# The last convolution block: where two squares stand in ScalarE's queue, and which engine makes two of its sums

## The chip, the cores and the metric

The kernel runs on one core of a Trainium2 chip. The core has TensorE (PE in the profile: matrix products into the accumulators called PSUM), VectorE (DVE), ScalarE (ACT), GpSimd (POOL) and SyncE (SP), each with an instruction queue of its own that it works off in order, and 16 DMA engines that move data between the chip's large memory and SBUF, the memory beside the engines. The metric is the time of one execution on the device in microseconds; with several runs, their median.

## The reference, cut to what matters

One layer of an encoder: 2048 positions, width 1024. Half of the projected columns are Fourier-mixed, the other half go through two gated long convolutions (Hyena).

```python
h = rmsnorm(x)
p = h @ w_in                       # 2048 x 2048: [Fourier 512 | x1 512 | x2 512 | v 512]
y_f = rmsnorm(real(fft2(p[:, :512] in 8 groups of 64)))
x1, x2, z = split(short_conv(p[:, 512:]))
for n, gate in enumerate((x1, x2)):
    z = gate * irfft(rfft(z, 4096) * k_freq[n])[:2048] + skip term
y_h = rmsnorm(z)
x = x + concat(y_f, y_h) @ w_out
x = x + relu(rmsnorm(x) @ w_fc1)**2 @ w_fc2
out = rmsnorm(x)
```

## The kernel before

The stages follow one another: input projection with the short convolution; the filters' spectra and the Fourier mix, both left in the chip's memory; the eight blocks of long convolutions (`hyena`, L744); the output projection (`project_out`); the two products of the feed-forward part. The change touches `hyena` and the class `Out`, which prepares the output projection.

**A convolution block.** A `Block(n, ct)` is the convolution `n` (two of them) of 128 of the 512 channels. The transform is done in two factors by matrix products. `first` makes the first factor and turns its result on VectorE. `second(q)`, q = 0 to 7, takes a group of four frequencies: it makes the second factor on TensorE into PSUM (L797) and multiplies by the filter's spectrum `ks`. A complex product needs the two halves of the rows swapped and one of them negated: ScalarE makes that swapped copy `zs` in two instructions (L800 the negated half, L801 the other). VectorE makes `y = p * ks[0]` (L803), GpSimd `zs = zs * ks[1]` (L804), and the two are summed into `y` (L805). In blocks 0 to 6 GpSimd makes the sums of q = 0 to 3 and VectorE those of q = 4 to 7; in the last block (number 7) GpSimd makes those of q = 0 and 1 and VectorE those of q = 2 to 7. `inverse(q)` multiplies `y` back on TensorE, and ScalarE copies the product into `V` (L814). `turn` turns `V` into `W` on VectorE, in eight pieces. `gate(q)` makes the last factor on TensorE (L826), and VectorE multiplies it by the gate `xg` into `zz` (L827).

**How blocks overlap.** In one pass over q, the block at hand goes through `second` and, three groups later (`LAG`), `inverse`; the block before it ends its `inverse` and is turned; the block before that is gated. Behind the loop the last block's inverse products of q = 5 to 7, the gates of block 6, and the turns and gates of block 7 are left.

**What is begun early for the output projection.** Behind `second(1)` of the last block, `Out.ahead` (L954, a generator that goes on at each `next`) loads the Fourier rows of two token tiles (`yf`, two transfers of 128 KB each per tile, L928 and L930), before the spectra of q = 4 to 7. Its second part is called at q = 7: for each of the two rows the mean of squares (`rms`, L237: the square on ScalarE at L240, with its sum read by a second, short instruction; then short steps on VectorE and a square root on ScalarE) and the scaling of the row on ScalarE (L962). Later parts transpose the rows on TensorE (L937), split them in two parts of reduced precision (`split`, L193 to L201; the cast `yh` on ScalarE, the rest `yl` on VectorE) and multiply them with `w_out` (L211 to L213). The weights of `w_out` (`ost`) are split on ScalarE and VectorE or GpSimd (`weights`, L911) before that. Their transfers take the buffers of the spectra that have been used.

**What sets the order.** The text above is not the order of the queues. The tile framework orders each engine's instructions itself when the program is built, from the dependences, the order of the text and a time model of its own; an instruction from further down may so come ahead. `behind(later, first)` (L203) adds an edge without a wait: `later` is placed behind `first` in the order. `squared` holds the last square that `rms` has issued. Before the change nothing ties the two squares of the Fourier rows to a place.

Of the kernel before, what the change touches and what calls it, by code (L numbers as in the profile page):

```python
# [134 lines left out]
def hybrid_block(ctx: ExitStack, tc: tile.TileContext, A, out):  # L135
    nc = tc.nc
# [36 lines left out]
    def pa(nm):  # L173
        banks["n"] += 1
        pl, tag = (ps, "a") if banks["two"] or banks["n"] % 2 else (banks["other"], "b")
        return pl.tile([P, 512], F32, tag=tag, name=nm, bufs=4)
# [26 lines left out]
    def behind(later, first):  # L203

        order = mybir.DependencyInfo(mybir.DependencyClass.NoSync, mybir.DependencyReason.DATA)
        for x in later:
            tc.add_manual_dep(x.ins, first.ins.name, order, reason="queue order")
# [7 lines left out]
    def rsqrt(v, pl, nm, keep=None, s=None):  # L215

        r = pl.tile(list(v.shape), F32, tag=f"rc_{nm}", name=f"rc_{nm}")
        q = pl.tile(list(v.shape), F32, tag=f"nw_{nm}{keep or ''}", name=f"nw_{nm}", bufs=keep)
        if s is None:
            s = pl.tile(list(v.shape), F32, tag=f"sq_{nm}", name=f"sq_{nm}")  # L220
            nc.scalar.sqrt(s, v)
        nc.vector.reciprocal(r, s)
        if v.shape[1] == 1:

            nc.vector.tensor_scalar(out=q, in0=r, scalar1=r, scalar2=v, op0=ALU.mult, op1=ALU.mult)
            nc.vector.tensor_scalar(out=q, in0=q, scalar1=-0.5, scalar2=1.5, op0=ALU.mult, op1=ALU.add)
            nc.vector.tensor_scalar(out=q, in0=q, scalar1=r, scalar2=None, op0=ALU.mult)
            return q
        nc.vector.tensor_mul(q, r, r)
        nc.vector.tensor_mul(q, q, v)  # L230
        nc.vector.tensor_scalar(out=q, in0=q, scalar1=-0.5, scalar2=1.5, op0=ALU.mult, op1=ALU.add)
        nc.vector.tensor_mul(q, r, q)
        return q

    squared = []

    def rms(src, width, junk, nm, keep=None):  # L237

        ssq = small.tile([P, 1], F32, tag="ssq", name=f"ssq_{nm}")
        squared[:] = [nc.scalar.activation(junk, src, AF.Square, accum_out=ssq)]  # L240
        v = small.tile([P, 1], F32, tag="var", name=f"v_{nm}")
        nc.vector.tensor_scalar(out=v, in0=ssq, scalar1=1.0 / width, scalar2=EPS, op0=ALU.mult, op1=ALU.add)
        return rsqrt(v, small, "s", keep)
# [106 lines left out]
    def doubled(i, q):  # L350

        both = kd[i // 2][i % 2].rearrange("h p s x -> h (p s) x")[:, :, 1024 * q : 1024 * q + 1024]
        behind([nc.sync.dma_start(both[1], both[0])], fetched[0])
# [390 lines left out]
    def hyena(hp, wp, rp, zz, e1, b1, f2, a2, work):  # L744
# [6 lines left out]
        class Block:  # L751
# [41 lines left out]
            def second(self, q):  # L793
                ks = self.ahead.pop(q) if q in self.ahead else self.spectrum(q)
                p = pa("pz2")
                for j in range(4):
                    nc.tensor.matmul(p[:, 128 * j : 128 * j + 128], lhsT=f2[q // 4][:, 4 * (q % 4) + j, :], rhs=self.G[:, :, 4 * q + j], start=True, stop=True)  # L797
                p3 = p.rearrange("p (f c) -> p f c", f=4)
                zs = hp.tile([P, 4, 128], F32, tag="zs", name="zs", bufs=4)
                nc.scalar.mul(zs[0:64], p3[64:128], -1.0)  # L800
                nc.scalar.copy(zs[64:128], p3[0:64])  # L801
                y = hp.tile([P, 4, 128], F32, tag="y", name="y", bufs=5)
                nc.vector.tensor_mul(y, p3, ks[:, 0])  # L803
                nc.gpsimd.tensor_mul(zs, zs, ks[:, 1])  # L804
                (nc.gpsimd if q in ((0, 1) if self is blocks[7] else (0, 1, 2, 3)) else nc.vector).tensor_add(y, y, zs)  # L805
                self.y[q] = y

            def inverse(self, q):
# [12 lines left out]
            def gate(self, q):  # L821
# [6 lines left out]
                    zz[:, 4 * q : 4 * q + 4, self.cs], p.rearrange("p (t c) -> p t c", t=4), self.xg[:, 4 * q : 4 * q + 4, :]  # L828
                )

        LAG = 3
        TURNS = ((0,), (1,), (2, 3), (4, 5), (6, 7))
        LAST = ((0,), (1, 2), (3, 4), (5, 6), (7,))
        FIRSTS = ((0, 1), (2, 3), (4,), (5,), (6,), (7,), (), ())
        blocks = [Block(n, ct) for n in range(2) for ct in range(4)]
# [7 lines left out]
        for i in range(8):  # L843
            cur, old, older, new = (blocks[j] if 0 <= j < 8 else None for j in (i, i - 1, i - 2, i + 1))
            for q in range(8):
                if new and q == 7:
                    new.ahead[0] = new.spectrum(0)
                cur.second(q)
                if older and q == 1:
                    for k in range(4):  # L850
                        older.gate(k)
                if old:
                    if q < LAG:
                        old.inverse(8 - LAG + q)
                    else:
                        for c in (TURNS if new else LAST)[q - LAG]:
                            old.turn(c)
                if q >= LAG:
                    cur.inverse(q - LAG)
                if old and q == 3:  # L860
                    old.load()
                if i == 7:
                    if q == 1:
                        cur.ahead.update((k, cur.spectrum(k)) for k in range(2, 4))
                        ahead = work.ahead(hp, cur.y[0][:, 0, 0:1])
                        next(ahead)
                        cur.ahead.update((k, cur.spectrum(k)) for k in range(4, 8))
                    elif q == 5:
                        for k in range(4):
                            work.load(hp, k)  # L870
                    elif q == 7:
                        next(ahead)
                    elif q == 6:
                        cur.load()
                if new:
                    for c in FIRSTS[q]:
                        new.first(c)
                if 1 <= i < 5 and q % 2:
                    doubled(SINGLE[i - 1], q // 2)
        old, older = blocks[7], blocks[6]  # L880
        for q in range(8 - LAG, 8):
            old.inverse(q)
        for k in range(0, 4):
            work.weights(hp, k)
        for q in range(4):
            older.gate(q)
        next(ahead)
        for c in range(8):
            old.turn(c)
# [10 lines left out]
    class Out:  # L900
# [53 lines left out]
        def ahead(self, hp, late):  # L954

            rows, fronts = [], []
            for t in tokens[0:2]:
                rows.append(self.fourier_rows(t, hp, "yf", 2, late))
            yield
            for y in rows:  # L960
                junk = hp.tile([P, 512], BF16, tag="yjunk", name="yjunk")
                nc.scalar.mul(y, y, rms(y, 512, junk, "f"))  # L962
            yield
            for t, yn in zip(tokens, rows):
                fronts.append(self.parts(yn, *(hp.tile([P, 4, P], F32, tag="y", name=n, bufs=5).bitcast(FR) for n in ("yh", "yl")), t))
            yield
            for t, f in zip(tokens, fronts):
                self.begun[t] = [pa("po") for _ in range(2)]
                for h in range(2):
                    self.multiply(self.begun[t][h], f, 0, h)  # L970
                yield
# [573 lines left out]
    with pool("raws") as rp:  # L1545
        with pool("wts") as wp:
            work = Out(wp, zp, zz, gy)
            with pool("hyena") as hp:
                hyena(hp, wp, rp, zz, e1z, b1, f2h, f2, work)
            tabs.close()  # L1550

            raws = rp.tile([P, 32, 128], F32, tag="W", name="W").rearrange("p (n f) c -> p n (f c)", n=4)
            b = {}
            with pool("op") as op:
                first = project_out(op, work, raws, b)
            with pool("fc1") as mp:
                begun = fc1(mp, raws, zp, b, *first)
        zstack.close()
# [55 lines left out]
```

## Time and profile before

| | |
|---|---|
| median of 3 runs | 2241.47 us (2239.9 to 2246.95) |
| the profiled execution: its time | 2239.05 us |
| the profiled execution: its span, first to last instruction | 2237.3 us |
| mean TensorE clock granted | 0.996 |
| busy share of the span | PE 98%, DVE 66%, ACT 48%, POOL 34% |
| the last block's `second`, q = 0 to its last sum | about 756 to 780.5 us |

The page gives busy times by engine over the whole span, the same in 40 slices, the DMA queues, a chain of waits, the costliest groups of instructions and the transfers' issues. The time lines quoted below give start, duration, engine, line, operation and tiles, how many instructions were merged (x2), and in brackets the idle time of that engine just before and what ended it. Durations of neighbouring instructions overlap a little, since one begins while the other's last results are written; where a queue is full, the difference of two starts is the time that an instruction takes.

### The profile page before, as it was taken

How to read it: one execution, taken by the hardware profiler on the slowest of the kernel's cores; microseconds unless marked ns; L12 is line 12 of the kernel's file. 1: busy time of each engine (PE TensorE's matmuls, PEld its weight loads, DVE VectorE, ACT ScalarE, POOL GpSimd, SP SyncE). 2: the span in 40 equal slices, each digit the busy share in tenths (PEclk: the TensorE clock that was granted, in tenths of full speed). 3: DMA queues.
4: the chain of work that ended last, by engine and by line, in shares of the span. 5: the costliest groups of instructions: out<-in, count | busy, mean ns of one | idle time of the engine just before them, and what ended most of it. 6: DMA issues, size and time to landing. Idle time of an engine off the chain costs nothing. (4 is left out here: it accounts for less than half of the span.)

```text
span 2237.3 us, 34489 instructions
## 1 busy us (share of the span) xinstructions
PE 2192.4 (98%) x12881; PEld 1793.3 (80%) x12881; DVE 1468.4 (66%) x2192; ACT 1072.4 (48%) x1783; POOL 762.3 (34%) x576
## 2 busy tenths in 40 slices
PE   8999899999999999999999999999999999999998
PEld 6888778676888778887888878888888888888886
DVE  6998767776788764467444464444476666866667
ACT  6554211355555654546555565555443333533333
POOL 3444323465366511327555446555200000000000
PEclk9999999999999999999999999999999999999999
DMA  8534797569998756586444465444498756866631
GB/s 266 177 134 159 268 335 295 191 218 350 314 306 260 234 161 183 169 265 211 155 156 155 155 238 167 153 146 151 160 381 297 242 188 197 305 194 189 199 111 76
DMA packets 287001, 475.95 MB, mean 213 GB/s; under 512 B 17573, under 2 KB 131439, under 8 KB 282097
## 3 DMA queue, kind: packets, MB, share of 16 engines
q1 hardware_dynamic: 280593, 458.22, 61.5%
q10 hardware_dynamic: 6240, 15.53, 2.1%
q8 instruction: 101, 1.65, 0.3%
q14 instruction: 67, 0.55, 0.1%
HBM read 312.51 MB, written 168.00 MB: 215 GB/s over the span
## 5 line engine op out<-in xcount | busy, mean ns | idle before, releaser
L197 ACT CAST qahm<-ra 128x1024 fp32r<-128x1024 f32 x110 | 115.9, 1053 | 345.0 <-PE p2u L212 171.7
L197 DVE TENSOR_TENSOR qalm<-ra,qahm 128x1024 fp32r<-128x1024 f32 x110 | 134.7, 1224 | 153.4 <-ACT qahm L197 151.7
L1379 POOL TENSOR_TENSOR acc<-acc,gfin 128x512 f32<-128x512 f32 x4 | 5.1, 1282 | 630.2 <-DMA out<-acc 624.4
L212 PE MATMUL pu<-wl,xh 128*128 128x512 f32 x512 | 201.9, 394 | 6.9 <-DVE wl L197 6.5
L211 PE MATMUL pu<-wh,xh 128*128 128x512 f32 x512 | 204.9, 400 | 2.6 <-ACT wh L201 2.6
L213 PE MATMUL pu<-wh,xl 128*128 128x512 f32 x512 | 201.8, 394 | 2.7 <-DVE xl L197 2.7
L212 PE MATMUL p2u<-qblm,qahm 128*128 128x512 f32 x504 | 196.1, 389 | 0.0
L211 PE MATMUL p2u<-qbhm,qahm 128*128 128x512 f32 x504 | 195.8, 389 | 0.0
L213 PE MATMUL p2u<-qbhm,qalm 128*128 128x512 f32 x504 | 195.8, 389 | 0.0
L197 DVE TENSOR_TENSOR qblm<-rb,qbhm 128x1024 fp32r<-128x1024 f32 x110 | 134.0, 1218 | 2.2 <-ACT qbhm L197 2.2
L421 POOL TENSOR_TENSOR acc<-acc,cw 128x512 f32<-128x512 f32 x45 | 60.9, 1354 | 197.5 <-DVE acc L398 194.3
L212 PEld LDWEIGHTS pu<-wl,xh 128*128 128x128 f32 x512 | 97.4, 190 | 28.8 <-DVE wl L197 6.9
L197 ACT CAST ahm<-s 128x512 fp32r<-128x512 f32 x120 | 74.4, 621 | 94.1 <-PE p1v L212 54.8
L197 ACT CAST qbhm<-rb 128x1024 fp32r<-128x1024 f32 x110 | 115.3, 1048 | 4.4 <-DMA rb<-in_w_fc 2.9
L213 PEld LDWEIGHTS pu<-wh,xl 128*128 128x128 f32 x512 | 97.2, 190 | 24.4 <-DVE xl L197 4.1
L211 PEld LDWEIGHTS pu<-wh,xh 128*128 128x128 f32 x512 | 97.4, 190 | 23.8 <-ACT wh L201 3.5
L197 POOL TENSOR_TENSOR alm<-W,ahm 128x512 fp32r<-128x512 f32 x60 | 83.3, 1390 | 86.8 <-ACT ahm L197 86.8
L211 PEld LDWEIGHTS p2u<-qbhm,qahm 128*128 128x128 f32 x504 | 94.6, 188 | 20.1 <-issue 0.3
L213 PEld LDWEIGHTS p2u<-qbhm,qalm 128*128 128x128 f32 x504 | 94.6, 188 | 19.8
L212 PEld LDWEIGHTS p2u<-qblm,qahm 128*128 128x128 f32 x504 | 94.6, 188 | 19.5
L1155 DVE TENSOR_TENSOR c<-p1v,ku 128x512 f32<-128x512 f32 x64 | 44.2, 690 | 89.9 <-ACT ku L1225 51.2
L197 POOL TENSOR_TENSOR alm<-s,ahm 128x512 fp32r<-128x512 f32 x60 | 92.2, 1537 | 29.6 <-ACT ahm L197 29.6
(379 smaller groups left out, 6148.9 us busy)
## 6 DMA issues: line engine op xcount, KB each, us to landing
ks<-spec SPq DMA_DIRECT2D x64, 512.0 KB
W<-in_w_fc SPq DMA_DIRECT2D x64, 512.0 KB
rb<-td SPq DMA_DIRECT2D x64, 512.0 KB
ra<-a1m SPq DMA_DIRECT2D x56, 512.0 KB
ra<-a0m SPq DMA_DIRECT2D x54, 512.0 KB
rb<-in_w_fc SPq DMA_DIRECT2D x46, 512.0 KB
f<-in_w_fc SPq DMA_DIRECT2D x16, 1024.0 KB
td<-f SPq DMA_DIRECT2D x16, 1024.0 KB
```

Of the source, the lines that this page charges most:

```text
L197: return nc.scalar.copy(hi, src), eng.tensor_sub(lo, src, hi)
L211: a = nc.tensor.matmul(o, lhsT=lh, rhs=rh, start=start, stop=False, skip_group_check=more)
L212: nc.tensor.matmul(o, lhsT=lh, rhs=rl, start=False, stop=False, skip_group_check=more)
L213: return a, nc.tensor.matmul(o, lhsT=ll, rhs=rh, start=False, stop=stop, skip_group_check=more)
L421: nc.gpsimd.tensor_add(m1, m1, cw[:, 3, :])
L1155: read["DVE"] = nc.vector.tensor_add(c, p, other)
L1379: nc.gpsimd.tensor_mul(acc[i][:, c], acc[i][:, c], gfin[:, c])
```

## The change

In the last block the sums of q = 3 and 5 go from VectorE to GpSimd as well (four on GpSimd, four on VectorE). And the two squares of the Fourier rows are tied behind the second half (L801) of the swapped copy of q = 6: `swapped` holds the copy that `second` issued last, the loop notes it at q = 6, and at q = 7 it places both squares behind it. `ahead` therefore collects both squares in `squared`. Nothing else changes; no transfer and no product is added or left out.

```diff
-                nc.scalar.copy(zs[64:128], p3[0:64])
+                swapped[:] = [nc.scalar.copy(zs[64:128], p3[0:64])]
...
-                (nc.gpsimd if q in ((0, 1) if self is blocks[7] else (0, 1, 2, 3)) else nc.vector).tensor_add(y, y, zs)
+                (nc.gpsimd if q in ((0, 1, 3, 5) if self is blocks[7] else (0, 1, 2, 3)) else nc.vector).tensor_add(y, y, zs)
...
+        swapped = []
...
+                    elif q == 6:
+                        last = swapped[0]
+                        cur.load()
                     elif q == 7:
                         next(ahead)
-                    elif q == 6:
-                        cur.load()
+                        behind(squared, last)
...
+            both = []
             for y in rows:
                 junk = hp.tile([P, 512], BF16, tag="yjunk", name="yjunk")
                 nc.scalar.mul(y, y, rms(y, 512, junk, "f"))
+                both += squared
+            squared[:] = both
```

## The prediction

> **What bounds the kernel now.** I read the page first, for the shares of the engines; then TensorE's waits behind the changed stage; then the time line of each engine in the last convolution block (about 752 to 805 us), since the diff touches nothing else.
>
> ```profile
> span 2237.3 us, 34489 instructions
> PE 2192.4 (98%) x12881; PEld 1793.3 (80%) x12881; DVE 1468.4 (66%) x2192; ACT 1072.4 (48%) x1783; POOL 762.3 (34%) x576
> ```
>
> TensorE (PE) is the bound of the whole: 2237.3 less 2192.4 leaves 45 us in which it does nothing, and no edit of order can win more than the part of these 45 us that lies where it acts. The change removes no matmul. So the question is which idle time of PE in the last block depends on ScalarE (ACT), VectorE (DVE) and GpSimd (POOL). First the stall that the change is aimed at, in the time line of ACT, DVE, POOL and PE (start, duration, engine, line, what; in brackets the idle time before and what ended it):
>
> ```profile
> 762.55 1.06 PE L797 MATMUL pz<-G,f2h 128*128 128x128 f32 x8
> 762.75 0.60 ACT L814 COPY V<-pv 128x512 f32<-128x512 f32 x1 [1.94 <-PE pv L813]
> 765.94 0.63 ACT L240 ACTIVATE yjunk<-yf 128x512 bf16<-128x512 f32 x1 [2.59 <-DMA yf<-yfd]
> 766.69 0.59 ACT L800 ACTIVATE zs<-pz 64x512 f32<-64x512 f32 x1
> 767.29 0.58 ACT L801 COPY zs<-pz 64x512 f32<-64x512 f32 x1
> 766.70 0.15 DVE L242 TENSOR_SCALAR v_f<-ssq_f 128x1 f32<-128x1 f32 x1 [4.33 <-ACT yjunk L240]
> 767.90 0.69 DVE L803 TENSOR_TENSOR y<-pz,ks 128x512 f32<-128x512 f32 x1 [1.05 <-ACT zs L801]
> 767.95 1.29 POOL L804 TENSOR_TENSOR zs<-zs,ks 128x512 f32<-128x512 f32 x1 [4.86 <-ACT zs L801]
> 770.11 1.13 PE L813 MATMUL pv<-y,f 128*128 128x128 f32 x8 [1.14 <-DVE y L805]
> ```
>
> The product of the third group of frequencies (q = 2) is ready on PE at 762.55 + 1.06 = 763.61. ACT, which must negate and swap its halves (L800, L801), stands from 763.35 to 765.94 before the square of a Fourier row whose transfer has not landed. So 765.94 - 763.61 = 2.33 us are lost for ACT; DVE and POOL, which wait for the swapped copy, lose 4.33 and 4.86 us, and PE, which had run ahead, pays 1.14 us at 770.11 and more after it.
>
> Next, the end of the stage:
>
> ```profile
> 768.50 0.62 ACT L240 ACTIVATE yjunk<-yf 128x512 bf16<-128x512 f32 x1
> 769.22 0.59 ACT L800 ACTIVATE zs<-pz 64x512 f32<-64x512 f32 x1
> 777.23 0.58 ACT L801 COPY zs<-pz 64x512 f32<-64x512 f32 x1
> 787.17 0.60 ACT L197 CAST yh<-pt_y 128x512 fp32r<-128x512 f32 x1
> 779.86 0.65 DVE L805 TENSOR_TENSOR y<-y,zs 128x512 f32<-128x512 f32 x1
> 781.06 1.16 PE L813 MATMUL pv<-y,f 128*128 128x128 f32 x8
> 787.82 0.50 PE L211 MATMUL po<-G,yh 128*128 128x512 f32 x1 [0.76 <-ACT yh L197]
> 790.20 3.07 DVE L492 STREAM_TRANSPOSE W<-V 128x512 f32<-128x512 f32 x5
> 793.52 1.94 PE L826 MATMUL pb<-W,b 128*64 128x512 f32 x8
> core 0: us, PE busy (x) PEld busy (x) DVE busy (x) ACT busy (x) POOL busy (x), PEclk, DMA share, GB/s
> 766.00:787.00 21.00, 17.16 (x115) 12.43 (x113) 18.54 (x37) 20.65 (x35) 9.71 (x7) 1.00 0.81 268
> ```
>
> From 766 to 787 ACT is busy for 20.65 of 21.00 us: after its stall it never waits again until the first cast of a transposed Fourier row (787.17), and PE's first output product starts right behind that cast, 0.76 us late. This full queue of ACT is the bound here. The other chain ends earlier: the last sum on DVE (779.86 + 0.65 = 780.51), PE's last inverse product (781.06), block 6's gates.
>
> **The change, part by part.** *Squares behind the seventh swapped copy.* Nothing is removed. Each square takes ACT's queue for 0.75 and 0.72 us (765.94 to 766.69, 768.50 to 769.22), 1.47 us together; they now come behind the copy of q = 6. The negated copy of q = 2 then starts when PE has its product, at 763.61 instead of 766.69, 3.1 us earlier; those of q = 3 to 6 are 2.33 + 1.47 = 3.8 us earlier; that of q = 7 is 2.33 us earlier with both squares ahead of it (775.5 for the end of its copy instead of 777.23 + 0.58 = 777.8), and up to 3.8 if the scheduler puts them behind it. I take 2.33. The rows have landed long before, so the squares wait for no transfer in their new place. What is late next is ACT's own list: its work from 765.94 to 787.17, 21.2 us, begun at 763.61, ends at 784.8, and the yh cast comes 2.33 us earlier. The scale factors that the rows need (three short DVE steps, then ACT) are made late in any case, behind the sums:
>
> ```profile
> 780.50 0.13 DVE L242 TENSOR_SCALAR v_f<-ssq_f 128x1 f32<-128x1 f32 x1
> 784.97 0.20 DVE L227 TENSOR_SCALAR nw_s<-nw_s,rc_s 128x1 f32<-128x1 f32 x1
> 784.99 1.36 ACT L962 ACTIVATE yf<-yf,nw_s 128x512 f32<-128x512 f32 x2
> ```
>
> The second row's mean square is read at 780.50, 11 us after its square (768.50 + 0.62), so squares that end some 4 us later, near 774, cost nothing there unless DVE's order changes (a rival, below).
>
> *Two sums from DVE to POOL.* The groups of operations between 760 and 790 us (count; busy time, mean ns; idle time before them):
>
> ```profile
> L804 POOL TENSOR_TENSOR zs<-zs,ks 128x512 f32<-128x512 f32 x7 | 9.2, 1314 | 8.3 <-ACT zs L801 7.7 <-DVE G L492 0.6
> L805 DVE TENSOR_TENSOR y<-y,zs 128x512 f32<-128x512 f32 x6 | 4.1, 685 | 0.0
> L492 DVE STREAM_TRANSPOSE G<-V 128x512 f32<-128x512 f32 x8 | 5.6, 703 | 0.0
> L805 POOL TENSOR_TENSOR y<-y,zs 128x512 f32<-128x512 f32 x2 | 2.6, 1280 | 0.2
> ```
>
> From 767.90 to 780.51 DVE issues 20 large operations without a pause (6 products, 8 turns, 6 sums): 12.6 us, 0.63 each. Two fewer save 1.26 us of DVE; its list, begun at 764.8, would be through at 764.8 + 11.35 = 776.2, so DVE is no longer the bound. POOL gets 2 x 1.28: six products and two sums are 6 x 1.314 + 2 x 1.28 = 10.4 us, from 764.8 to 775.2, beside a last product that cannot start before 775.5. So POOL can hold it, with little room; each sum itself comes 1.28 - 0.69 = 0.6 us later than on DVE. Its readers are the inverse products of q = 3 and 5. The last sum (q = 7, still on DVE) ends at 775.5 + 1.31 + 0.65 = 777.5 instead of 780.51: 3.0 us earlier. That is 0.7 us more than ACT's gain, and the smaller of the two counts: **2.3 us**.
>
> *Transfers.* No new ones; but faster readers could run into them.
>
> ```profile
> 763.40 2.71 SPq L776 DMA_DIRECT2D ks<-spec  x4
> 766.00:772.00 6.00, 4.86 (x43) 4.64 (x41) 4.21 (x8) 5.86 (x13) 2.58 (x2) 1.00 1.01 345
> ```
>
> The spectra of q = 4 to 7, 512 KB each, are issued just behind the Fourier rows. With the rows landed at 765.94 and 345 GB/s, 1.52 us each, they land at my estimate at 767.5, 769.0, 770.5 and 772.0. The swapped copies would be there at 768.5, 770.3, 772.2 and 775.5, so the spectra are 1.0 to 3.5 us early. I cost them at nothing; without that cover the chain of the sums has 0.7 us of slack.
>
> *What follows.* The stage's later steps (turns to 793.27, gates at 793.52, output products) hang on the yh cast and on the last inverse product and shift as a whole. TensorE's largest waits from 803 us on are these (us in total, times, longest):
>
> ```profile
> PE p1u L211 <- ACT ku L1225: 2.1, 3, 1.0
> PE p1u L211 <- ACT bm L197: 1.6, 1, 1.6
> PE po L211 <- ACT oyh L197: 0.9, 2, 0.7
> ```
>
> None is for a transfer directly; all are for work that follows PE's own results, so nothing there should swallow the gain. Sum: 2239.05 us of the profiled execution less 2.3 is 2236.7. That execution lies 2.4 us below the median of the three runs (2241.47); the middle of all four executions (2239.05, 2239.9, 2241.47, 2246.95) is 2240.7, and I forecast **2240.7 - 2.3 = 2238.4 us**.
>
> **Rivals.** *DVE and POOL block each other* (the gain goes). The trace has the row:
>
> ```profile
> 610.14 2.96 POOL L804 TENSOR_TENSOR zs<-zs,ks 128x512 f32<-128x512 f32 x2 [1.26 <-DVE y L803]
> 610.15 1.81 DVE L805 TENSOR_TENSOR y<-y,zs 128x512 f32<-128x512 f32 x1
> ```
>
> A DVE sum of two SBUF operands that starts 0.01 us behind a POOL product takes 1.81 us instead of 0.69, 1.1 more. In the block as it is, POOL pauses (8.3 - 4.86) / 6 = 0.57 us before a product, and DVE's sums fall into those pauses (mean 685 ns). With POOL nearly full, the four sums left on DVE have few pauses: at worst 4 x 1.1 = 4.5 us, DVE through at 780.7, the gain of the sums' chain gone. It decides from 0.7 us on, so from the first blocked sum; two of them leave 2.3 - 1.5 = 0.8 us. Result between 2239.9 and 2240.9. For it speaks POOL's 10.4 us in a stretch of 12; against it, that the two moved sums are two fewer that can be blocked. The Trainium skill, in "SBUF — State Buffer" under "Who interferes with whom", says that a DVE instruction with two SBUF inputs and a GpSimd instruction that reads SBUF share one read interface, and that the later one waits for the whole of the first; in "Perfetto Trace Analysis", under "Optimizing Scalar/DVE Operations", it concludes that moving work between the two might not help. The row at 610.15 agrees with the first; by that rule the result is this rival's.
>
> *Slower: the rows' scaling falls behind the turns.* The squares now end near 774, and their short DVE steps may be queued behind the eight turns of the last block instead of ahead of them. These turns end at 793.27 now, near 791 in the forecast. PE's first output products (787.82 to 793.5, 5.6 us) now run beside the turns; they would come after, with a scaling, a transpose and a cast ahead of them (0.7 + 0.7 + 0.6). PE would reach the gates of 793.52 at 791 + 2.0 + 5.6 = 798.6, 5.1 us late: 2245.8. It decides at once: the output products end (793.5) just when the turns do, so each us by which the scaling is later than 784.99 - 2.33 = 782.7 costs one. Against it: even now the steps wait 11 us on DVE and still come ahead of the turns, and DVE is free from 777.5 on.
>
> *More than forecast.* The squares go behind the copy of q = 7 and the yh casts ahead of two weight casts: up to 3.8 + 0.76 = 4.6 us, 2236.1.
>
> *The change does not do what it says.* The copy noted at q = 6 is that of the seventh group, and both squares are tied to it; only the scheduler's choice behind it is open, which the other cases hold.
>
> **How the numbers follow.** Forecast 0.58, blocked ports 0.22, more than forecast 0.11, scaling behind the turns 0.09. Runs scatter from 2239.05 to 2246.95, so 0.3% (6.7 us) is about what a measurement can tell from no change. The range, 2235 to 2243.5, holds the forecast with its scatter, the blocked ports and most of the larger gain; it leaves out the slow case. Faster than 2234.7 needs the larger gain and a lucky median: 0.07. Slower than 2248.2 needs the slow case and a bad one: 0.04. Within: 0.89.
>
> **What would show it.** Right: ACT's negated copy of q = 2 directly behind PE's product; no wait of ACT for the Fourier row; the squares between the copy of q = 6 and the weights; DVE's last sum at about 777.5; yh cast near 784.8; PE's first output product near 785.5 and the gates near 791.2. Wrong: DVE sums or POOL products of 1.5 us and more; POOL waiting for a spectrum; the scaling behind the turns; or PE at 805 us ahead by 2.3 us and the end not.

## The result and the profile after

| | before | after |
|---|---|---|
| median of 22 executions each | 2241.15 us (2236.6 to 2246.95) | 2245.28 us (2239.3 to 2249.85) |
| ratio, 95% interval | | 1.0025 [1.0018, 1.0032] |
| the profiled execution: time, span, mean clock | 2239.05, 2237.3 us, 0.996 | 2244.74, 2242.9 us, 0.995 |

By the interval the change costs 4 to 7 us where 2.3 us were to be won; the medians differ by 4.1 us. Single executions of one kernel lie up to 10 us apart, so the profiles are compared by stretches and not by their spans. From the page of after:

```profile
span 2242.9 us, 34496 instructions
PE 2193.4 (98%) x12881; PEld 1793.7 (80%) x12881; DVE 1468.9 (65%) x2190; ACT 1072.6 (48%) x1783; POOL 760.9 (34%) x578
```

The span is 5.6 us longer than before. PE is busy for 1.0 us more (2193.4 instead of 2192.4 us), and 4.6 us are more idle time of PE. All marks below are counted from one point that the change cannot move, the start of the negated copy of q = 1 in the last block. First that row of before, and one row of its tail that is needed later:

```profile
758.33 0.60 ACT L800 ACTIVATE zs<-pz 64x512 f32<-64x512 f32 x1
787.80 0.69 DVE L197 TENSOR_TENSOR yl<-pt_y,yh 128x512 fp32r<-128x512 f32 x1 [0.21 <-ACT yh L197]
```

Then the time lines of ACT, POOL, DVE and PE of after, in the block:

```profile
758.99 0.59 ACT L800 ACTIVATE zs<-pz 64x512 f32<-64x512 f32 x1
764.35 0.59 ACT L800 ACTIVATE zs<-pz 64x512 f32<-64x512 f32 x1 [0.34 <-PE pz L797]
779.47 0.29 ACT L221 ACTIVATE sq_s<-v_f 128x1 f32<-128x1 f32 x2 [2.32 <-DVE v_f L242]
781.24 1.32 ACT L966 ACTIVATE yf<-yf,nw_s 128x512 f32<-128x512 f32 x2
783.17 0.59 ACT L814 COPY V<-pv 128x512 f32<-128x512 f32 x1 [0.61 <-PE pv L813]
788.67 0.58 ACT L197 CAST yh<-pt_y 128x512 fp32r<-128x512 f32 x1
770.08 2.52 POOL L804 TENSOR_TENSOR zs<-zs,ks 128x512 f32<-128x512 f32 x2
773.89 1.28 POOL L805 TENSOR_TENSOR y<-y,zs 128x512 f32<-128x512 f32 x1 [1.29 <-DVE y L803]
771.40 1.74 DVE L805 TENSOR_TENSOR y<-y,zs 128x512 f32<-128x512 f32 x1 [0.61 <-POOL zs L804]
773.07 0.68 DVE L803 TENSOR_TENSOR y<-pz,ks 128x512 f32<-128x512 f32 x1
776.45 1.74 DVE L805 TENSOR_TENSOR y<-y,zs 128x512 f32<-128x512 f32 x1 [0.30 <-POOL zs L804]
779.49 0.69 DVE L805 TENSOR_TENSOR y<-y,zs 128x512 f32<-128x512 f32 x1
778.33 1.34 PE L813 MATMUL pv<-y,f 128*128 128x128 f32 x8 [1.95 <-DVE y L805]
```

The aim is reached: the copy of q = 2 starts right behind PE, 764.35 - 758.99 = 5.36 us behind the mark instead of 766.69 - 758.33 = 8.36, and nothing waits for a Fourier row. But the last sum ends at 779.49 + 0.69 - 758.99 = 21.19 instead of 780.51 - 758.33 = 22.18: 1.0 us earlier and not 3.0. Two DVE sums take 1.74 us; behind the first of them stands the product that POOL's sum of q = 5 waits for (773.07), and so POOL stands for 1.29 us. ACT, relieved of its 2.59 us, stands for 2.32 and 0.61 us further on.

And the tail of after, PE and DVE:

```profile
789.30 0.50 PE L211 MATMUL po<-G,yh 128*128 128x512 f32 x1 [1.56 <-ACT yh L197]
789.64 0.40 PE L212 MATMUL po<-G,yh 128*128 128x512 f32 x1
792.08 0.50 PE L213 MATMUL po<-G,yl 128*128 128x512 f32 x1 [2.05 <-DVE yl L197]
792.65 0.52 PE L212 MATMUL po<-G,yh 128*128 128x512 f32 x1
793.40 0.63 PE L211 MATMUL po<-V,yh 128*128 128x512 f32 x1
795.96 0.50 PE L211 MATMUL po<-G,yh 128*128 128x512 f32 x1
798.92 0.65 PE L826 MATMUL pb<-W,b 128*64 128x512 f32 x2
788.97 2.48 DVE L492 STREAM_TRANSPOSE W<-V 128x512 f32<-128x512 f32 x4
791.38 0.65 DVE L197 TENSOR_TENSOR yl<-pt_y,yh 128x512 fp32r<-128x512 f32 x1
```

DVE's queue has another order than before. There the first `yl` came behind one turn and 0.03 us behind its cast (787.80); now it stands behind four turns, ends at 792.03, and PE waits 2.05 us for it. From PE's first output product to the gates of the last block it is 798.92 - 789.30 = 9.62 us instead of 793.52 - 787.82 = 5.70. A second loss lies in the same stretch; stretches of 2 us of after (length, then the busy us of PE, PEld, DVE, ACT, POOL with counts, granted clock, DMA share, GB/s):

```profile
778.99:780.99 2.00, 2.00 (x7) 0.67 (x5) 2.00 (x12) 1.52 (x4) 0.00 (x0) 0.53 0.50 126
792.99:794.99 2.00, 2.00 (x6) 1.61 (x5) 2.00 (x5) 0.25 (x1) 0.04 (x1) 0.50 0.78 227
```

TensorE's granted clock falls twice to about half. From 792.65 to 795.96 PE takes 3.31 us for eight matmuls that take 8 x 0.23 = 1.84 us at the full clock (0.23 us from start to start, as in before), 1.5 us more.

The marks of all profiles (us from the start of the copy of q = 1; the differences of the starts, for the last sum of its end), with the measured ratios and whether the clock fell in this stretch:

| | last sum | `yh` cast | gates | clock | ratio, 95% |
|---|---|---|---|---|---|
| before | 22.18 | 28.84 | 35.19 | full | |
| after | 21.19 | 29.68 | 39.93 | falls twice | 1.0025 [1.0018, 1.0032] |
| squares alone | 20.85 | 28.10 | 34.77 | falls | 1.0002 [0.9993, 1.0010] |
| sums alone | 24.69 | 33.31 | 40.34 | falls | 1.0016 [1.0008, 1.0025] |
| change, DVE's order as before | 21.18 | 28.91 | 36.33 | full | 1.0003 [0.9992, 1.0014] |
| change, DVE's and ACT's order as before | 21.18 | 28.93 | 35.25 | full | 0.9999 [0.9987, 1.0010] |
| squares alone, DVE's order as before | 21.92 | 30.31 | 36.60 | falls | 0.9998 [0.9988, 1.0008] |
| before, `yl` late | 22.35 | 29.01 | 36.64 | full | 1.0003 [0.9992, 1.0014] |
| change, orders as before, products first | 18.96 | 27.09 | 34.98 | falls | 0.9999 [0.9989, 1.0009] |
| squares early, sums as before | 19.87 | 27.01 | 33.36 | full | 0.9992 [0.9982, 1.0002] |
| before, again | 21.62 | 28.27 | 34.61 | full | |
| after, again | 21.19 | 28.92 | 38.31 | falls once | 1.0020 [1.0011, 1.0030] |
| squares early, again | 19.92 | 27.07 | 33.41 | full | 0.9995 [0.9983, 1.0006] |
| squares early, four sums on GpSimd | 20.30 | 28.52 | 34.88 | falls | 1.0002 [0.9993, 1.0011] |

### The profile page after: what moved, and what is told of

The parts are those of the page before. It is cut to its first block, busy times and chain, and to the rows that moved or that the text cites. A ratio compares the mean times of both kernels' runs of the same rounds, so it can differ in the third digit from the quotient of the medians.

```text
span 2242.9 us, 34496 instructions
## 1 busy us (share of the span) xinstructions
PE 2193.4 (98%) x12881; PEld 1793.7 (80%) x12881; DVE 1468.9 (65%) x2190; ACT 1072.6 (48%) x1783; POOL 760.9 (34%) x578
## 3 DMA queue, kind: packets, MB, share of 16 engines
q8 instruction: 101, 1.65, 0.3%
## 5 line engine op out<-in xcount | busy, mean ns | idle before, releaser
L211 PE MATMUL p1u<-bm,ahm 128*128 128x512 f32 x252 | 98.9, 392 | 3.9 <-ACT ku L1231 2.3
```

The lines of the kernel that those rows point to most:

```text
L211: a = nc.tensor.matmul(o, lhsT=lh, rhs=rh, start=start, stop=False, skip_group_check=more)
```

## The experiments

**The two halves of the change.** The squares' tie without the two moved sums, and the sums without the tie:

```diff
-  (nc.gpsimd if q in ((0, 1, 3, 5) if self is blocks[7] else ...
+  (nc.gpsimd if q in ((0, 1) if self is blocks[7] else ...
```
```diff
-                        behind(squared, last)
+                        pass
```

> The change's first part alone: both squares tied behind the swapped copy of q = 6, all sums on the engines of before. Theory A (order of the tail: in the changed kernel ACT's square roots stand ahead of the weight casts and wait 2.3 us for VectorE, and the yl splits stand behind four and six of the eight turns, for which TensorE waits 2.05 us): here the roots stand behind the two weight casts and the first yl behind three turns, so most of the loss is absent: time of before less 0 to 2 us. Theory B (squares at this place are what costs, since the scaling of the rows comes later): as slow as the changed kernel, +4 to +6 us. Theory C (GpSimd and VectorE block each other): faster than before by about 2 us, for GpSimd has no sums more.

> The change's second part alone: the sums of q = 3 and 5 on GpSimd, the squares where they were. Theory A: the tail keeps nearly the order of before (yl behind two and three turns, roots behind the weight casts): within 1.5 us of before. Theory B: as before, within 0.5 us, or up to 1.3 us faster. Theory C: slower than before by 2 to 5 us, with sums on VectorE of 1.7 us in the trace.

The squares alone change nothing that can be measured (1.0002); the sums alone lose, 1.0016 [1.0008, 1.0025]. So it is the sums that can lose by themselves. The halves do not simply add up, though: with the sums alone the last sum comes 2.5 us later than before, in the whole change 1.0 us earlier, so the loss of the whole change must arise behind the sums. In the profile of the sums alone, POOL, DVE and PE:

```profile
774.78 2.51 POOL L804 TENSOR_TENSOR zs<-zs,ks 128x512 f32<-128x512 f32 x2
778.58 1.28 POOL L805 TENSOR_TENSOR y<-y,zs 128x512 f32<-128x512 f32 x1 [1.29 <-DVE y L803]
776.09 1.74 DVE L805 TENSOR_TENSOR y<-y,zs 128x512 f32<-128x512 f32 x1 [0.78 <-POOL zs L804]
781.13 1.74 DVE L805 TENSOR_TENSOR y<-y,zs 128x512 f32<-128x512 f32 x1 [0.28 <-POOL zs L804]
783.02 2.05 PE L813 MATMUL pv<-y,f 128*128 128x128 f32 x8 [1.95 <-DVE y L805]
```

The same two blocked sums and the same wait of POOL: they come from the sums and not from the squares. PE's product of 783.02 takes 2.05 us and not 1.13: the clock is at half here too, so part of the 5.15 us that this profile loses up to the gates is the clock's.

In the profile of the squares alone POOL waits for a spectrum:

```profile
768.19 4.38 POOL L804 TENSOR_TENSOR zs<-zs,ks 128x512 f32<-128x512 f32 x3 [1.39 <-DMA ks<-spec]
771.38 1.74 DVE L805 TENSOR_TENSOR y<-y,zs 128x512 f32<-128x512 f32 x1
```

ACT's copies are 3 us earlier, the spectrum of q = 4 is not; POOL then works off three products in a row, and a DVE sum beside them is blocked. Of 3.0 us the last sum keeps 1.3, the cast 0.7, the gates 0.4; the clock is at half in this profile from 775.3 to 778.7, and how much of the difference is the clock's is not shown.

**The order behind the block.** The change as it is, with DVE's order in the tail tied to that of before (the gates of block 6 behind the rests of two weights, `yl` ahead of the second and of the fourth turn); then with ACT's as well (the two roots behind the second weight's cast):

```diff
+        lows = [work.weights(hp, k)[1] for k in range(0, 4)]
+        gated = [older.gate(q) for q in range(4)]
+        behind(gated, lows[1])
...
+        behind(turns[1:], parted[0][1])
+        behind(turns[3:], parted[1][1])
```
```diff
+        behind(rooted, heads[1][0])
```

Here `parted` holds the pairs `yh`, `yl` of the two rows, `heads` the two instructions of each weight, and `rooted` the roots of the two rows.

> The whole change, with VectorE's order behind the block put back by ties: the first two weight rests ahead of block 6's gates, the first yl split behind one turn of block 7, the second behind three. ACT keeps its order (roots ahead of the weight casts). Theory A: TensorE's wait of 2.05 us for yl goes, the weights' next transfers start earlier; the wait of ACT for the roots (2.3 us) stays: 2 to 4 us faster than the changed kernel, that is +1.5 to +3.5 us against before. Theory B: the scaling is as late, so as slow as the changed kernel within 1 us. Theory C: as slow within 1 us, the two blocked sums stay.

> As the run before, and ACT's two square roots are tied behind the cast of the second weight, where the second one stood in the kernel before; so the tail has the order of before on both engines, and the whole change stands. Theory A: the loss is gone: before less 1 to 2.5 us. Theory B: the scaling comes no earlier, so +3 us or more. Theory C: the two blocked sums (2 x 1.1 us) stay and with them +2 us or more.

DVE's order takes 39.93 - 36.33 = 3.6 us of the loss away (wait for `yl` and low clock together; 2.0 against the second profile of after, below, in which the clock falls only once), ACT's 1.1 more, and the measured loss goes with them: 1.0003, then 0.9999; both intervals hold 1. With both orders back the change is worth nothing: gates at 35.25, before 35.19. ACT in that profile:

```profile
782.06 0.60 ACT L816 COPY V<-pv 128x512 f32<-128x512 f32 x1 [2.34 <-PE pv L815]
```

The stall of 2.59 us that the squares' new place removed is there again, as 2.34 us in front of PE's inverse product, which waits for the late sums. That is where the forecast gain went. The cast stands at the same mark in both profiles, 28.91 and 28.93, whether the roots are ahead of the weights' casts or behind: what holds it up is the late sums, and for the cast the place of the roots only decides at which instruction ACT waits for them.

The reverse, before with only `yl` moved behind four and six turns (here `parted` holds the `yl` alone), and the squares alone with DVE's order tied as above:

```diff
+        behind(parted[0:1], turns[3])
+        behind(parted[1:2], turns[5])
```

> The kernel before, with nothing of the change, but with the yl splits of the two Fourier rows tied behind the fourth and the sixth turn of block 7, where they stand in the changed kernel. Theory D: TensorE waits 2 to 3 us for them; the gates of block 7 start 2 to 4 us later, the run is 2 to 4 us slower than before. If the place of yl does not matter, within 0.5 us of before.

> The squares tied behind the copy of q = 6, the sums on the engines of before, and the tail's order of before on VectorE (yl splits behind one and three turns, weight rests ahead of block 6's gates). Theory D (now held: the two sums on GpSimd lengthen the chain of the sums, by sums that block each other and by a GpSimd sum that waits for VectorE's product; and the new order of the tail adds the rest): like the squares alone, 0.3 to 1.5 us faster than before; the last block's gates start 0.4 to 1.5 us earlier, counted from the swapped copy of q = 1. Theory B (the late squares cost): slower than before.

`yl` behind its turns costs 1.45 us at the gates, less than expected, and is not seen in the time: 1.0003 [0.9992, 1.0014], an interval that 1.45 us (1.0006) would fit as well. PE in that profile:

```profile
794.79 0.50 PE L211 MATMUL po<-G,yh 128*128 128x512 f32 x1 [0.76 <-ACT yh L197]
795.59 0.40 PE L212 MATMUL po<-G,yh 128*128 128x512 f32 x1
796.98 0.50 PE L213 MATMUL po<-G,yl 128*128 128x512 f32 x1 [0.99 <-DVE yl L197]
```

PE waits 0.99 us and not 2.05, and the clock stays up. PE's own order differs too: here, as in before, four products of the casts (794.79 to 795.99) stand ahead of the first one with `yl`, in after only two (789.30 and 789.64). So the place of `yl` on DVE is not the whole loss. The squares alone with DVE's order came out at 0.9998; their profile has the clock down from 782 to 789 and shows nothing of the order.

**Undoing the blocked chain.** The change with both orders tied and, on DVE, the products of q = 5 and 7 ahead of the sums of q = 4 and 6:

```diff
+        behind([old.y[4, 1]], old.y[5, 0])
+        behind([old.y[6, 1]], old.y[7, 0])
```

> The whole change with the tail's order of before on both engines (as in the fourth run), and in addition VectorE's products of q = 5 and 7 are placed ahead of its sums of q = 4 and 6. Theory D: GpSimd no longer waits 1.3 us for the product of q = 5, the last sum ends 1 to 2 us earlier than in the fourth run (21.2 us behind the swapped copy of q = 1 there), and the gates of block 7 0.5 to 2 us earlier than before. If blocking alone is the price, the last sum moves by less than 0.5 us.

Last sum 18.96, 3.2 us earlier than before and 2.2 earlier than with the orders alone, and cast 27.09, 1.75 earlier than before: the forecast's step for the sums is there and most of that for the cast. POOL no longer waits for DVE's product (the cross wait), but the sums are also blocked for less. POOL and DVE:

```profile
772.85 1.61 POOL L807 TENSOR_TENSOR y<-y,zs 128x512 f32<-128x512 f32 x1
772.15 1.17 DVE L807 TENSOR_TENSOR y<-y,zs 128x512 f32<-128x512 f32 x1
776.28 1.82 DVE L807 TENSOR_TENSOR y<-y,zs 128x512 f32<-128x512 f32 x2
```

One sum takes 1.17 us and the other two 1.82 us together, where the version with both orders tied has 1.75, 1.74 and 0.69. So the edit takes away the cross wait and about half of the blocking at once; how the 2.2 us divide between the two is not shown. The gates are only 0.2 earlier than before. PE and two stretches:

```profile
787.50 0.63 PE L211 MATMUL po<-G,yh 128*128 128x512 f32 x1
790.85 0.39 PE L213 MATMUL po<-V,yl 128*128 128x512 f32 x1
```
```profile
783.94:787.35 3.41, 1.76 (x10) 1.28 (x11) 2.21 (x5) 3.41 (x6) 3.11 (x2) 1.00 0.25 102
787.14:789.14 2.00, 2.00 (x6) 1.53 (x6) 2.00 (x4) 2.00 (x3) 1.83 (x1) 0.55 0.67 178
```

PE reaches the output products early, having stood for 3.41 - 1.76 = 1.65 of 3.41 us, and runs most of the first ones at half the clock: eight steps from 787.50 to 790.85 are 3.35 us instead of 1.84, 1.5 us lost.

**Squares still earlier.** The sums as before, the squares behind the copy of q = 2, DVE's order tied, the fifth and sixth weight's casts behind the rows' casts, and their rests behind the last turn:

```diff
+                    elif q == 2:
+                        last = swapped[0]
                     elif q == 6:
-                        last = swapped[0]
                         cur.load()
...
+            behind([rest[j][0]], parted[j][0])
+            behind([rest[j][1]], turns[7])
```

> Nothing of the sums' change; the squares tied behind the swapped copy of q = 2 instead of q = 6 (so that no swapped copy waits for the Fourier rows), with the tail's order of before. Theory D: the swapped copy of q = 2 starts 3 us earlier, as in the change; the last sum 1 to 2 us earlier than before, the gates of block 7 0.5 to 2 us earlier: time 0.5 to 2 us less than before. If ScalarE's stall was covered by other waits, as slow as before within 0.5 us.

The best of all: cast and gates 1.83 us earlier than before. Its rows, ACT, DVE and PE:

```profile
763.83 0.59 ACT L800 ACTIVATE zs<-pz 64x512 f32<-64x512 f32 x1 [0.34 <-PE pz L797]
777.68 0.65 DVE L805 TENSOR_TENSOR y<-y,zs 128x512 f32<-128x512 f32 x1
785.47 0.59 ACT L197 CAST yh<-pt_y 128x512 fp32r<-128x512 f32 x1
791.82 1.94 PE L826 MATMUL pb<-W,b 128*64 128x512 f32 x8
```

All six sums take 0.65 to 0.69 us, since POOL keeps its pauses.

**Order or clock: the same kernels again.** Before, after and the last version a second time, unchanged, and a version with the squares early, four sums on GpSimd, products first and all orders tied:

> The kernel before itself, for a second profile. Theory A (order and waits alone set the stage; the granted clock of TensorE is noise of the single run): the marks behind the swapped copy of the second group repeat within 0.3 us (last sum 22.2, first cast of a transposed row 28.8, gates of the last block 35.2). Theory B (the clock falls in this stage by chance of phase): the last sum repeats, but the gates may come up to 1.6 us later, with matmuls of 0.63 us in place of 0.39 in the profile.

> The changed kernel itself, a second profile and a second measurement. Theory A (its loss is the order: blocked sums, square roots ahead of the weights' casts, low parts of the rows behind four and six turns): last sum 21.2, cast 29.7, gates 39.9 as in the first profile, within 0.3 us, and ratio 1.002 to 1.003. Theory B (1.4 us or more of its loss is the clock that fell in the first profile, by chance of phase): the gates come at 38.3 to 38.6 when the clock stays at 1.00, and at 39.9 when it falls; the ratio lies between 1.001 and 1.003.

> The version with the squares behind the third swapped copy, the sums as before and the order of the tail written out, measured again. Theory A: gates at 33.4 again, 1.8 us earlier than before, ratio 0.9992 within 0.0010. Theory B: the cast again at 27.0, the gates at 33.4 or, with the clock down, near 35.0; ratio 0.9992 to 1.0000.

> The change's two sums on GpSimd, but the products of the sixth and eighth group ahead of the sums of the fifth and seventh on VectorE (so that GpSimd doesn't wait), the squares behind the third swapped copy, the roots behind the second weight's cast, the fifth and sixth weight's casts behind the rows' casts. Theory A: the third group is again 3 us earlier, last sum at 19.0 to 19.9, cast at 27.0, gates at 33.0 to 33.4, ratio 0.9990 to 0.9993. Theory B: the same cast, but with TensorE idle for longer ahead of it the clock falls and the gates come near 35.0: ratio 0.9998 to 1.0003.

After loses again, 1.0020 [1.0011, 1.0030], but its gates come at 38.31 and not 39.93: the first fall of the clock is missing, the second is there. PE, and a stretch:

```profile
779.30 1.13 PE L813 MATMUL pv<-y,f 128*128 128x128 f32 x8 [1.94 <-DVE y L805]
791.47 0.76 PE L213 MATMUL po<-G,yl 128*128 128x512 f32 x1 [1.23 <-DVE yl L197]
```
```profile
792.00:794.00 2.00, 2.00 (x6) 1.58 (x5) 2.00 (x5) 0.52 (x1) 0.83 (x1) 0.50 0.69 236
```

The waits are the same in both profiles to 0.01 us up to the last sum (1.94 and 1.95), the clock is not. So the waits belong to the kernel, and the place of a fall to the single execution; the last section shows on what it hangs. "Squares early" repeats to 0.06 us and to 0.9995 [0.9983, 1.0006]; its two intervals both reach 1, so its 1.83 us are shown in the profile and not in the time. Before, of which this is a single execution (2234.34 us), came a little earlier than the first time, for a reason that fits the forecast's ACT term:

```profile
760.66 0.63 ACT L240 ACTIVATE yjunk<-yf 128x512 bf16<-128x512 f32 x1 [2.03 <-DMA yf<-yfd]
```

The row landed 2.59 - 2.03 = 0.56 us earlier, and cast and gates are 0.57 and 0.58 us earlier: here a us of ACT's stall is a us of the stage, as far as one pair of profiles can show it. The last version missed its 27.0 for the cast. ACT there, and a stretch:

```profile
784.09 0.59 ACT L817 COPY V<-pv 128x512 f32<-128x512 f32 x1 [1.10 <-PE pv L816]
```
```profile
782.00:784.00 2.00, 2.00 (x13) 1.78 (x11) 2.00 (x4) 0.61 (x2) 0.00 (x0) 0.50 0.57 91
```

At half the clock PE's inverse products keep ACT waiting. Even without the cross wait, four sums on GpSimd came out no better (1.0002) than two (0.9992 and 0.9995).

## Why the prediction was wrong

- **ACT's stall: right.** The copy of q = 2 comes 3.0 us earlier, that of q = 7 3.1 (at least 2.33 forecast), and no wait for a Fourier row is left. That a us of this stall is a us at the cast fits the second profile of before (0.56 and 0.57).
- **"POOL can hold it, with little room": the first step that failed.** The forecast cast up POOL's busy time and did not ask when DVE's sums are released. A sum on DVE is released by POOL's product; with POOL's queue full, POOL's next product starts at that moment, so the sum is blocked for the whole of it: 1.74 us instead of 0.69, twice. Between them stands the product that POOL's own sum needs, 1.29 us more. Of 3.0 us the last sum kept 1.0. The rival "block each other" named the mechanism and left 0.8 us of gain; the order-tied change shows none (gates +0.06), because ACT's stall came back behind PE (2.34 us). "Products first" took the cross wait and about half of the blocking away and had 3.2 us, which shows the step, though not which of the two weighs more.
- **"ACT's own list" as the bound up to the cast: wrong from the squares on.** The scheduler drew the two roots ahead of the weights' casts, and ACT stood 2.32 us for their mean squares, which DVE makes behind its blocked sums. The cast came 0.84 us late in the first profile of after and 0.08 in the second, not 2.33 early. With the roots put back it came no earlier (28.93 and 28.91): ACT's list is not the bound while the sums that it waits for come late.
- **"Hang on the yh cast and on the last inverse product and shift as a whole": the step that made a loss of it.** They don't: from the first output product to the gates it is 9.62 and, in the second profile, 8.76 us instead of 5.70. In the first profile, the gap between the starts 789.64 and 792.08 is 2.44 us instead of 0.23, so 2.2 us are the wait for `yl`; 1.5 us are the clock. With the order tied back the loss is gone (1.0003 and 0.9999), which shows that it hangs on the order. How the 3.6 us of DVE's order divide between wait and clock differs from one execution to the next.
- **The slower rival** had the right shape and the wrong victim: not the scaling, which starts at 22.3 us behind the mark instead of 26.7, but `yl` went behind the turns. Its price of 5.1 us was near what was measured (4.1 us between the medians, 4.7 at the gates of the first profile), which is luck: it was summed for another path. It got 0.09, because only the scaling was looked at.
- **Spectra "1.0 to 3.5 us early": wrong** where nothing else holds the chain up: POOL waited 1.39 us for that of q = 4 with the squares alone.
- **The starting point** of 2240.7 us was good: 2241.15. But the 0.3% that a measurement was said to tell from no change were read from single executions; the medians of 22 tell 0.07%, so that a loss of 0.25% was seen.

Still open is how the loss of 4 to 7 us divides between PE's wait for `yl`, PE's own order and the clock: the place of `yl` alone cost 1.45 us at the gates.

## What to carry to other kernels

Work moved to an engine that shares operands with its neighbour is priced by who releases whom, not by busy time: an engine whose queue closes up blocks exactly the instruction that its last result has released. Where a framework orders the queues, an edit at one place is followed by a look at the order of everything queued behind it, since a cheap instruction that slips behind four others can cost more than the edit was to win. And a wait of TensorE may cost more than its length, when the clock falls behind it, as it did here behind windows in which TensorE was busy for less than about half.

## What the runs showed of the hardware

**The clock of TensorE falls without a long pause, behind a window that is about half empty.** It fell to half in 7 of the 14 profiles of this stage, eight times in all: for 3.41 us six times and for 6.83 us twice. The longest gap between matmuls in these seven is 2.38 us. In each profile all changes of the clock, from the program's start to its end, lie on one grid of 3.413 us: in after the first fall begins at 779.11 and the second at 792.76, four steps later. Where this grid lies against the stage differs from one execution to the next. PE in windows of the grid, two of after and then two of the second profile of after:

```profile
775.70:779.11 3.41, 1.46 (x14) 1.30 (x13) 3.11 (x4) 1.45 (x4) 1.94 (x2) 1.00 1.13 328
789.35:792.76 3.41, 1.36 (x5) 0.84 (x6) 3.41 (x7) 2.29 (x3) 3.41 (x2) 1.00 0.79 193
```
```profile
777.89:781.30 3.41, 2.00 (x10) 1.16 (x10) 3.41 (x9) 1.09 (x5) 0.72 (x1) 1.00 0.93 240
788.13:791.54 3.41, 0.80 (x3) 0.37 (x3) 3.41 (x7) 3.03 (x5) 3.41 (x2) 1.00 0.64 179
```

Behind those with 1.46, 1.36 and 0.80 us the clock falls. The second profile of after has the waits of the first one here too (0.80 and 1.94 us), but its grid cuts between them: PE is busy for 2.00 us and the clock stays. Over all 14 profiles, from 20 to 2225 us, the full clock fell behind 47 windows, in which PE was busy for 51.5% at most, and stayed behind 8909, in which it was busy for 47% at least; so the border is near half. In both profiles of before and of "squares early" PE is busy for at least 56% of any 3.41 us of the stage, so no position of the grid makes such a window; in after nearly every position does (of 200 counted). With both orders tied three positions in four do, and yet no loss was measured, so a fall alone does not cost what after lost.

The Trainium skill, in "TensorE: Matmul & The Clock Gate" under "What's actually happening", says that the gate passes half or all of the clock, judged over a free-running window of about 3.4 us, and falls behind an idle window. The half (0.43 us from matmul to matmul instead of 0.23), the window of 3.413 us and its running free agree; that a window must be idle does not, since PE was busy for 43% and 40% of the two ahead of the falls of after.

**A blocked sum waits for the whole of the other instruction.** In after the sum of 771.40 starts with POOL's second product (770.08 to 772.60) and ends at 773.14, 0.54 us behind it. With the products first, DVE's sum of 772.15 is ahead of POOL's of 772.85, and POOL's takes 1.61 us instead of 1.28. That agrees with what the Trainium skill states in "SBUF — State Buffer" under "Who interferes with whom": of a VectorE instruction with two inputs in SBUF and a GpSimd one that reads SBUF, the one that starts first keeps the shared read interface for its whole length, and the other is blocked.
